# A layer step on one core: first product behind the second transposes, row factors inside the first unit's product, x differences on VectorE

## Chip, cores and metric

The kernel runs on one core of one Trainium2 chip. The metric is the device time of one execution in microseconds; three runs of the kernel before gave 2393.43, 2394.09 and 2395.15 us, so its median is 2394.09 us. One more execution was taken by the hardware profiler, and all rows that are shown come from it.

The engines are named as the profile names them: PE (TensorE matmuls, with PEld for its weight loads), DVE (VectorE), ACT (ScalarE), POOL (GpSimd) and SP (SyncE, which here only issues DMAs). A name with a q behind it (SPq, ACTq) is the engine's instruction queue.

## What is computed

One layer of a hybrid encoder over 512 prompt frames and 64 sample frames, so T = 576 frames of width 2048:

```python
hn = rmsnorm(x, g_norm1)
q, k, v, gb, gc, hc = split(hn @ w_in)           # 2048 x 6144
q, k = rmsnorm(q, g_q), rmsnorm(k, g_k)          # per head of 128
o_attn = stick_breaking(q, k, v)                 # 8 heads, cached keys for the sample
o_conv = gb * conv3_causal(gc * hc)
x = x + concat(rmsnorm(o_attn), rmsnorm(o_conv)) @ w_out
h2 = rmsnorm(x, g_norm2)
x = x + (silu(h2 @ w_gate) * (h2 @ w_up)) @ w_down
```

The outputs are x, the new key and value rows, and the last two rows of gc * hc. Everything is f32. Each f32 matmul is done as three matmuls of rounded halves (hi*hi, lo*hi, hi*lo), which is why every operand is split by a cast (ACT) and a subtraction (DVE).

## The kernel before

Frames lie along the free dimension in two halves of 288. The norm of the first layer is applied late: the products run on x times g_norm1 alone, and each result is multiplied by R1, a [128, 576] tile that holds 1/rms of every frame in all partitions ("row factors").

The change concerns the first 100 us, the input projection's start. It has three stages.

Stage one, the loop over `kt` from 0 to 18 (lines 674 to 704). For each of the 16 row blocks of x, `turn_x(kt)` turns the loaded x by four transposes on PE into a PSUM bank `psx` (banks z0 and z1 in turn), and the sample frames by small transposes into `psx_s` (bank "misc"); ACT copies them to `st`, and ACT and DVE make the hi and lo operands b11, b12 and bod, scaled by g_norm1 (`g1c`). `step0(0, v0ps, kt - LAG)` is the product of pass kt - 3: twelve matmuls, into four PSUM banks (three of "pj", one of z2), of the columns of two value heads. Its weights come in four quarters (`load_wv`), split by `split_wv`: a cast on ACT, a subtraction on DVE. `x_sums` (lines 574 to 588) makes four differences of x's quarters for the later products, three on DVE and one (t2) on POOL; `x_parts` splits them into t12a and t34a. `x_squares` sums the squares for the norm.

Stage two, the second loop over `kt` from 0 to 15 (lines 721 to 753): `step0(1, v1ps, kt)` for two further value heads, into banks z0, z1 and the two of "misc", beside what is left of x_squares, x_sums and x_parts. At kt 9 the squares become 1/rms (`rst`, a power on POOL); at kt 11 five diagonal tiles `dg` are made from it on DVE; at kt 13, ahead of that pass's matmuls in PE's order, `turn_vectors` turns the small vectors and five f32 matmuls of a matrix of ones with `dg` spread 1/rms over all partitions into `ps_r`, which DVE copies to R1.

Stage three, the units. A unit is a 256-column piece of a product, done by seven half-size products (numbers 1 to 7) from sums of weight quarters and sums of frame quarters. Weights of a unit come as two halves into raw_a and raw_b; `weight_sums` makes four sums of them on DVE (lines 348, 350, 352, 354), and `prepare` splits one operand `whl` by a cast on ACT (line 231) and a subtraction on DVE (line 232), four products ahead. `run(n, p)` does product p of unit n: 24 matmuls in eight steps, and after each step `pipe.tick()` lets waiting generators go on. `tokens` is such a generator: it turns a finished value tile E back into token rows by PE transposes into "misc" (tok_a, four transposes, then tok_b, one), copied by ACT and stored by SP. E0 and E1 are the value tiles of stages one and two, multiplied by R1 on DVE ahead of `tokens`. The first units are -22 and -21 (-NA and 1 - NA in the code), and the order of the first products is (-22,1), (-22,2), (-21,1), (-21,2), (-22,3), (-22,6), (-22,5).

What sets the order: PE's instructions stand in the order of the code throughout. In stages one and two ACT, DVE and SP do too. In stage three a scheduler orders ACT, DVE, POOL and SP when the kernel is built; each engine then runs its list in order. In the list of the kernel before, ACT copies the token rows of both E1 tiles ahead of the two `whl` casts that need the weight sums of lines 352 and 354. In the list of the changed kernel these two casts, and the cast of x_sums' b11, stand ahead of the first token copy, and the scaling of the two E0 tiles stands between the sums of lines 350, 352 and 354 on DVE.

Pools hand out their buffers in turn: "misc" has two, so the third token transpose waits until ACT has copied the first; "hl" has three, and holds the x differences and the token rows alike.

## Time and profile before

| | us |
|---|---|
| runs: median (lowest to highest) | 2394.09 (2393.43 to 2395.15) |
| the profiled execution | 2397.15 |
| its span, first to last instruction | 2395.4 |
| PE busy | 2350.2 (98%) |
| DVE busy | 1934.0 (81%) |
| ACT busy | 1234.6 (52%) |
| POOL busy | 300.3 (13%) |
| mean granted TensorE clock | 0.995 |

Timeline rows give the start, the duration, the engine, the line, the operation, the tile written and the tiles read, the shape, and how many instructions are merged; in brackets stands how long the engine had been idle before it and what ended that. Durations include the drain of an instruction, so the start of the next one on the same engine gives the pace. The rows of a table by stretches give, for each engine, the busy time and in brackets the instructions, then the granted TensorE clock, the share of the DMA engines, and GB/s.

### The profile page before, as it was taken

To read this page: it belongs to the slowest core of one execution; us is meant where nothing else is said; L and a number is where in the kernel's file an instruction comes from. 1 tells how busy PE (TensorE), PEld (TensorE's weight loads), DVE (VectorE), ACT (ScalarE), POOL (GpSimd) and SP (SyncE) were. 2 spreads that over 40 slices of the span, in tenths; PEclk is the share of its full clock that TensorE was granted. 3 is DMA by queue.
4 is the path that set the end of the run, shared out by engine and by line. 5 is a ranking of instruction groups with operands and counts; after the bars stand their busy time and mean duration, and the time that the engine had idled before them with its cause. 6 is when DMAs were issued, how large, how long until landed. Compare 5 with 4: busy or idle time off the path is not lost.

```text
span 2395.4 us, 43789 instructions
## 1 busy us (share of the span) xinstructions
PE 2350.2 (98%) x17609; PEld 2336.2 (98%) x17609; DVE 1934.0 (81%) x2828; ACT 1234.6 (52%) x2211; POOL 300.3 (13%) x377
## 2 busy tenths in 40 slices
PE   8899999999999999999999999999999899999998
PEld 8899999999899999999999999999999899999998
DVE  7888888787677768888888888888888768887875
ACT  7456656455777545444444444444444444444454
POOL 0111121120233221000000000000000002431211
PEclk9999999999999999999999999999999999999999
DMA  7433343525733333444444444345354936875642
GB/s 254 141 113 104 114 138 89 162 88 188 236 105 104 107 135 106 141 150 132 139 151 142 129 150 153 118 156 159 109 157 139 338 111 212 225 222 194 204 129 79
DMA packets 474900, 360.60 MB, mean 151 GB/s; under 512 B 11278, under 2 KB 460680, under 8 KB 474696
## 3 DMA queue, kind: packets, MB, share of 16 engines
q1 hardware_dynamic: 469528, 351.02, 45.8%
q0 software_dynamic: 5168, 6.79, 1.6%
q8 instruction: 138, 2.26, 0.4%
q14 instruction: 66, 0.54, 0.1%
HBM read 281.39 MB, written 76.37 MB: 149 GB/s over the span
## 4 chain that ended last, share of the span: by engine, by line
PE 82%; DVE 6%; ACT 4%; issue 2%; DMA 1%; POOL 1%; SPq 0%; DVEq 0%; ACTq 0%; POOLq 0%
PE psy L406 43%; PE psw L406 21%; PE psx L406 10%; PE pjo L227 5%; DVE whl L232 1%; DMA v_dram<-tok 1%; PE pw L1391 1%; ACT whl L231 1%; ACT ph L231 0%; PE pot L1514 0%; DVE c L881 0%; ACT whi L179 0%; DMA raw_a<-in_w_down_dram 0%; DVE raw_b L350 0%; DVE wlo L180 0%
## 5 line engine op out<-in xcount | busy, mean ns | idle before, releaser
L232 DVE TENSOR_TENSOR whl<-raw_a,whl 128x1024 fp32r<-128x1024 f32 (+4 forms) x376 | 424.6, 1130 | 70.2 <-ACT whl L231 68.5
L406 PE MATMUL psy<-t,whl 128*128 128x288 f32 x2916 | 437.3, 295 | 0.5 <-ACT part L429 0.5
L231 ACT CAST whl<-raw_a 128x1024 fp32r<-128x1024 f32 (+4 forms) x376 | 352.3, 938 | 141.4 <-PE psx L406 52.1
L406 PE MATMUL psy<-h_s,whl 128*128 128x288 f32 x2724 | 411.8, 295 | 6.8 <-ACT part L429 6.8
L406 PEld LDWEIGHTS psy<-t,whl 128*128 128x128 f32 x2916 | 403.4, 189 | 0.9 <-ACT part L429 0.7
L406 PEld LDWEIGHTS psy<-h_s,whl 128*128 128x128 f32 x2724 | 378.7, 189 | 7.3 <-ACT part L429 7.3
L406 PE MATMUL psw<-t,whl 128*128 128x288 f32 x2592 | 377.2, 295 | 0.0
L406 PEld LDWEIGHTS psw<-t,whl 128*128 128x128 f32 x2592 | 354.0, 189 | 0.2
L232 DVE TENSOR_TENSOR whl<-raw_b,whl 128x1024 fp32r<-128x1024 f32 (+5 forms) x230 | 247.7, 1077 | 89.3 <-ACT whl L231 87.8
L231 ACT CAST whl<-raw_b 128x1024 fp32r<-128x1024 f32 (+5 forms) x230 | 207.2, 903 | 208.2 <-PE psw L406 70.0
L429 ACT COPY part<-psy 128x288 f32<-128x288 f32 x303 | 120.8, 399 | 350.0 <-PE psy L406 345.4
L406 PE MATMUL psx<-h_s,whl 128*128 128x288 f32 x1122 | 166.8, 297 | 2.7 <-DVE gs L1371 2.7
L406 PEld LDWEIGHTS psx<-h_s,whl 128*128 128x128 f32 x1122 | 156.2, 191 | 2.9 <-issue 2.9
L231 ACT CAST whl<-s 128x1024 fp32r<-128x1024 f32 (+5 forms) x101 | 93.3, 924 | 119.9 <-PE psw L406 114.1
L406 PE MATMUL psy<-t12a,whl 128*128 128x288 f32 x1056 | 150.0, 295 | 2.0 <-ACT part L429 2.0
L406 PE MATMUL psw<-t34a,whl 128*128 128x288 f32 x1056 | 150.4, 295 | 1.4 <-DVE ghs L869 0.9
L406 PEld LDWEIGHTS psy<-t12a,whl 128*128 128x128 f32 x1056 | 143.2, 188 | 2.7 <-ACT part L429 2.7
L406 PEld LDWEIGHTS psw<-t34a,whl 128*128 128x128 f32 x1056 | 143.4, 188 | 1.9 <-DVE ghs L869 1.1
L232 DVE TENSOR_TENSOR whl<-s,whl 128x1024 fp32r<-128x1024 f32 (+5 forms) x101 | 107.5, 1065 | 19.9 <-ACT whl L231 18.1
L227 PE MATMUL pjo<-mixc,whi 128*128 128x288 f32 x512 | 119.4, 300 | 0.0
L1334 POOL DMA_DIRECT2D hid_dram<-form x3 | 2.4, 807 | 923.9 <-DVE form L232 923.9
L227 PE MATMUL pjo<-mixa,whi 128*128 128x288 f32 x512 | 102.7, 295 | 0.0
(599 smaller groups left out, 4138.4 us busy)
## 6 DMA issues: line engine op xcount, KB each, us to landing
hid_dram<-form SPq DMA_DIRECT2D x147, 288.0 KB, 2.3
raw_a<-in_w_gate_dram SPq DMA_DIRECT2D x23, 1024.0 KB, 6.4
raw_a<-in_w_up_dram SPq DMA_DIRECT2D x23, 1024.0 KB, 6.0
raw_a<-in_w_in_dram SPq DMA_DIRECT2D x22, 1024.0 KB, 5.5
raw_b<-in_w_in_dram SPq DMA_DIRECT2D x22, 1024.0 KB, 8.2
raw_b<-in_w_gate_dram SPq DMA_DIRECT2D x21, 1024.0 KB, 6.7
raw_b<-in_w_up_dram SPq DMA_DIRECT2D x21, 1024.0 KB, 7.8
h_s<-hid_dram SPq DMA_DIRECT2D x10, 2016.0 KB, 9.9
```

The source lines that it names most:

```text
L227: mm(ps, w_[:, k, csl], x_[:, a:b], start=(k == 0 and n == 0), stop=(k == nk - 1 and n == 2))
L231: cast = nc.scalar.copy(out=hi, in_=src)
L232: (lo_eng or nc.vector).tensor_tensor(out=lo, in0=src, in1=hi.bitcast(F32), op=ALU.subtract)
L406: mm(ps, whl[:, w_, j, :], x_, start=(start and j == 0 and q == 0), stop=(j == len(xs_) - 1 and q == 2), skip_group_check=True)
L429: nc.scalar.copy(out=t, in_=st["y"])
L1334: q.dma_start(out=hid_dram[fp][2 * n - 2 : 2 * n].rearrange("f p t -> p f t"), in_=t.bitcast(F32))
L1391: mm(pss[j, i], w_[:, k, j * P : (j + 1) * P], x_, start=(kk == 0 and k == 0 and n == 0), stop=(kk == 1 and k == 7 and n == 2))
```

## The change

The diff, cut to its core:

```diff
--- before.py
+++ after.py
...
@@ -531,10 +532,10 @@
...
-    def load_s(c):
+    def load_s(c, queue=nc.sync):
         t = tmp.tile([P, 2, HALF], F32, tag="hl", name="xsn", bufs=3).rearrange("p i t -> p (i t)")
         xsn[c] = t[:TS, : 4 * P]
-        nc.sync.dma_start(out=xsn[c], in_=xs[:, 4 * c * P : 4 * (c + 1) * P])
+        queue.dma_start(out=xsn[c], in_=xs[:, 4 * c * P : 4 * (c + 1) * P])
 
     stp = {}
     banks = {}
@@ -543,15 +544,19 @@
         j, q = divmod(kt, 2)
         c = next(c for c, (k0, k1) in enumerate(XCH) if k0 <= kt < k1)
         k = kt - XCH[c][0]
+        psx = ps_z.tile([P, 512], F32, tag=f"z{kt % 2}", name=f"psx{kt}")
+        for i in range(4):
+            nc.tensor.transpose(psx[:, i * P : (i + 1) * P], xin[c][:, i, k * P : (k + 1) * P], ident)
         if kt % 8 == 0:
             banks["s"] = misc("psx_s")
         if kt % 4 == 0:
             for s in range(4):
                 o = (kt % 8 + s) * TS
                 nc.tensor.transpose(banks["s"][:, o : o + TS], xsn[kt // 4][:, s * P : (s + 1) * P], ident[:TS, :TS])
-        psx = ps_z.tile([P, 512], F32, tag=f"z{kt % 2}", name=f"psx{kt}")
-        for i in range(4):
-            nc.tensor.transpose(psx[:, i * P : (i + 1) * P], xin[c][:, i, k * P : (k + 1) * P], ident)
+        if kt == 0:
+            psg = misc("ps_g1")
+            nc.tensor.transpose(psg[:, :KD], g1raw, ident[:KD, :KD])
+            nc.vector.tensor_copy(out=g1c, in_=psg[:, :KD])
         if q == 0:
             stp[j] = ypool.tile([P, 2, T], F32, tag=f"y{j}", name=f"st{j}")
         st = stp[j]
@@ -582,7 +587,7 @@
         ta, tb = (tmp.tile([P, 2, HALF], F32, tag=tag, name="tab", bufs=3 if tag == "hl" else 2) for _ in range(2))
         t1, t2, t3, t4 = ta[:, 0], ta[:, 1], tb[:, 0], tb[:, 1]
         nc.vector.scalar_tensor_tensor(out=t1, in0=ev[:, HALF:], scalar=ge, in1=b11s, op0=ALU.mult, op1=ALU.subtract)
-        nc.gpsimd.tensor_tensor(out=t2, in0=b22s, in1=t1, op=ALU.subtract)
+        nc.vector.tensor_tensor(out=t2, in0=b22s, in1=t1, op=ALU.subtract)
         nc.vector.scalar_tensor_tensor(out=t3, in0=ev[:, HALF:], scalar=ge, in1=b22s, op0=ALU.mult, op1=ALU.subtract)
         nc.vector.scalar_tensor_tensor(out=t4, in0=od[:, :HALF], scalar=go, in1=t2, op0=ALU.mult, op1=ALU.subtract)
         tabs[j] = ta, tb
@@ -623,22 +628,29 @@
         def raw0(q):
             return raw_tile["A"][:, q // 2, q % 2 * 1024 : (q % 2 + 1) * 1024]
 
-        def load_wv(v, q):
+        def load_wv(v, q, a=0, b=4):
             c0 = 2 * AW + 2 * v * P
-            nc.sync.dma_start(out=raw0(q).rearrange("p (k c) -> p k c", k=4),
-                              in_=w_in[4 * q * P : 4 * (q + 1) * P, c0 : c0 + 2 * P].rearrange("(k p) c -> p k c", p=P))
-
-        def split_wv(v, q):
-            if q % 2 == 0:
+            nc.sync.dma_start(out=raw0(q).rearrange("p (k c) -> p k c", k=4)[:, a:b],
+                              in_=w_in[(4 * q + a) * P : (4 * q + b) * P, c0 : c0 + 2 * P]
+                              .rearrange("(k p) c -> p k c", p=P))
+
+        def split_wv(v, q, a=0, b=4):
+            if q % 2 == 0 and a == 0:
                 wv[v, q // 2] = [wpool.tile([P, 2048], F32R, tag=tag, name=tag) for tag in ("whi", "wlo")]
-            hi, lo = (t[:, q % 2 * 1024 : (q % 2 + 1) * 1024] for t in wv[v, q // 2])
-            split(hi, lo, raw0(q))
+            a, b = 256 * a, 256 * b
+            hi, lo = (t[:, q % 2 * 1024 : (q % 2 + 1) * 1024][:, a:b] for t in wv[v, q // 2])
+            if v == q == a == 0:
+                nc.vector.tensor_copy(hi, raw0(q)[:, a:b])
+                nc.vector.tensor_tensor(out=lo, in0=raw0(q)[:, a:b], in1=hi.bitcast(F32), op=ALU.subtract)
+            else:
+                split(hi, lo, raw0(q)[:, a:b])
 
         load_x(0)
-        load_s(0)
-        nc.sync.dma_start(out=g1raw, in_=g_norm1[0].rearrange("(r c) -> r c", c=P))
+        load_s(0, nc.scalar)
+        nc.scalar.dma_start(out=g1raw, in_=g_norm1[0].rearrange("(r c) -> r c", c=P))
+        load_wv(0, 0, 0, 2)
         load_x(1)
-        load_wv(0, 0)
+        load_wv(0, 0, 2, 4)
         load_x(2)
         load_s(1)
         load_x(3)
@@ -674,11 +686,12 @@
         for kt in range(KD + LAG):
             if kt < KD:
                 if kt == 0:
-                    psg = misc("ps_g1")
-                    nc.tensor.transpose(psg[:, :KD], g1raw, ident[:KD, :KD])
-                    nc.vector.tensor_copy(out=g1c, in_=psg[:, :KD])
+                    split_wv(0, 0, 0, 2)
                 turn_x(kt)
-            if kt in (0, 4, 8, 12):
+                if kt == 1:
+                    split_wv(0, 0, 2, 4)
+                    step0(0, v0ps, 0)
+            if kt in (4, 8, 12):
                 split_wv(0, kt // 4)
             if kt in (2, 6, 10, 14):
                 square(xsn[kt // 4], ssx[:TS, 4, kt // 4 : kt // 4 + 1], nc.scalar)
@@ -700,8 +713,8 @@
                 x_sums(j, "e" if j < 2 else "hl")
             if kt in (9, 13):
                 x_parts((kt - 9) // 4)
-            if kt >= LAG:
-                step0(0, v0ps, kt - LAG)
+            if kt == 3 or kt > 4:
+                step0(0, v0ps, 1 if kt == 3 else kt - LAG)
         e0 = [e_tile(f"E0{c}") for c in range(2)]
         for c in range(2):
             for i, (a, b) in enumerate(HALVES):
@@ -710,8 +723,8 @@
                 else:
                     nc.vector.tensor_copy(out=e0[c][:, a:b], in_=v0ps[c][i])
         x_parts(2)
-        v1ps = [[ps_z.tile([P, 512], F32, tag=f"z{i}", name="pjz")[:, :HALF] for i in range(2)],
-                [misc("pjm")[:, :HALF] for i in range(2)]]
+        v1ps = [[(ps_z.tile([P, 512], F32, tag=f"z{c + 1}", name="pjz") if c == i else misc("pjm"))[:, :HALF]
+                 for i in range(2)] for c in range(2)]
         load_columns([("A", 0)])
         R1 = rpool.tile([P, T], F32, tag="R", name="R1", bufs=2)
 
@@ -729,28 +742,42 @@
                 nc.vector.reduce_sum(out=ssr, in_=ssx, axis=mybir.AxisListType.X)
                 nc.vector.tensor_scalar(out=ssr, in0=ssr, scalar1=1.0 / D, scalar2=EPS, op0=ALU.mult, op1=ALU.add)
                 nc.gpsimd.tensor_tensor(out=rst, in0=ssr, in1=nhalf, op=ALU.pow)
-            if kt in (2, 5, 8, 11, 14):
-                x_parts(3 + (kt - 2) // 3)
-            if kt == 11:
-                dg = [hl_tile("dg") for _ in range(2)]
-                dg = [dg[i // 4][:, i % 4 * P : i % 4 * P + n] for i, (_, n) in enumerate(row_pieces())]
-                for i, (_, n) in enumerate(row_pieces()):
-                    nc.vector.tensor_scalar(out=dg[i][:n], in0=ident[:n, :n], scalar1=rst[:n, i : i + 1], scalar2=None,
-                                            op0=ALU.mult)
-            if kt == 13:
-                turn_vectors(ps_pj.tile([P, 512], F32, tag="pj", name="ps_vec"))
-                psr = [ps_pj.tile([P, 512], F32, tag="pj", name="ps_r1") for _ in range(2)]
-                for i, (o, n) in enumerate(row_pieces()):
-                    mm(psr[i // 4][:, o % TP : o % TP + n], oner.bitcast(F32)[:n, :], dg[i][:n], start=True, stop=True)
-                nc.vector.tensor_copy(R1[:, :TP], psr[0])
-                nc.vector.tensor_copy(R1[:, TP:], psr[1][:, :TS])
-            if kt in (1, 4, 7, 10, 13):
+            if kt in (3, 6, 9, 12):
+                x_parts(3 + (kt - 3) // 3)
+            if kt in (1, 4, 7, 10):
                 x_sums(3 + (kt - 1) // 3, "hl")
             if kt == 10:
                 prepare(-NA, 1)
-            if kt == 15:
+            if kt == 13:
+                dg = hl_tile("dg")
+                for i, (o, n) in enumerate(row_pieces()):
+                    nc.vector.tensor_scalar(out=dg[:n, o : o + n], in0=ident[:n, :n], scalar1=rst[:n, i : i + 1],
+                                            scalar2=None, op0=ALU.mult)
                 prepare(-NA, 2)
             step0(1, v1ps, kt)
+
+    def first_scale():
+        yield 5
+        psr, psv = (ps_pj.tile([P, 512], F32, tag="pj", name=name) for name in ("ps_r1", "ps_vec"))
+        for i, (o, n) in enumerate(row_pieces()):
+            mm(psr[:, o : o + n] if i < 4 else psv[:, P : P + n], oner.bitcast(F32)[:n, :], dg[:n, o : o + n],
+               start=True, stop=True)
+        nc.vector.tensor_copy(R1[:, :TP], psr)
+        nc.vector.tensor_copy(R1[:, TP:], psv[:, P : P + TS])
+        e1 = [lpool.tile([P, UW - 2], F32, tag=f"c{c}", name="E1")[:, :T] for c in range(2)]
+        for c in range(2):
+            for i, (a, b) in enumerate(HALVES):
+                nc.vector.tensor_tensor(out=e1[c][:, a:b], in0=v1ps[c][i], in1=R1[:, a:b], op=ALU.mult)
+            pipe.spawn(tokens(e1[c], vp[:, 2 + c, :], vs[:, 2 + c, :], v_dram[2 + c], 8 + 5 * c))
+        turn_vectors(psv)
+        yield 6
+        x_sums(7, "hl")
+        yield 3
+        x_parts(7)
+        yield 12
+        for c in range(2):
+            nc.vector.tensor_tensor(out=e0[c], in0=e0[c], in1=R1, op=ALU.mult)
+            pipe.spawn(tokens(e0[c], vp[:, c, :], vs[:, c, :], v_dram[c], 8 + 8 * c))
 
     def tokens(E, dst, dst_s, dram, lag):
         yield lag
...
@@ -908,16 +934,9 @@
                                        op0=ALU.mult, op1=ALU.subtract)
         nc.sync.dma_start(out=mixc_dram[g][:, :, a:b], in_=m.bitcast(F32))
 
-    e1 = [lpool.tile([P, UW - 2], F32, tag=f"c{c}", name="E1")[:, :T] for c in range(2)]
-    for c in range(2):
-        for i, (a, b) in enumerate(HALVES):
-            nc.vector.tensor_tensor(out=e1[c][:, a:b], in0=v1ps[c][i], in1=R1[:, a:b], op=ALU.mult)
-        pipe.spawn(tokens(e1[c], vp[:, 2 + c, :], vs[:, 2 + c, :], v_dram[2 + c], 4 + 5 * c))
+    pipe.spawn(first_scale())
     raw_tile["B"] = lpool.tile([P, 2, 2048], F32, tag="rb", name="raw_b")
     load_columns([("B", 0), ("B", 1)])
-    for c in range(2):
-        nc.vector.tensor_tensor(out=e0[c], in0=e0[c], in1=R1, op=ALU.mult)
-        pipe.spawn(tokens(e0[c], vp[:, c, :], vs[:, c, :], v_dram[c], 24 + 8 * c))
 
     order = [(-NA, 1), (-NA, 2), (1 - NA, 1), (1 - NA, 2), (-NA, 3), (-NA, 6), (-NA, 5), (1 - NA, 3), (-NA, 7), (-NA, 4),
              (1 - NA, 6), (1 - NA, 5), (1 - NA, 7), (2 - NA, 1), (1 - NA, 4), (2 - NA, 2), (2 - NA, 6), (2 - NA, 7),
```

On PE, `psx` is turned ahead of `psx_s`, and the turning of g_norm1 moves behind both. On SP the first x_sample load and g_norm1 are gone (ACT's queue issues them), and the first weight quarter comes in two pieces. On DVE the first half of that quarter is split whole, ahead of g1c; the t2 of all eight `x_sums` is done there instead of on POOL. Passes 0 and 1 of the first product stand behind the transposes of row blocks 1 and 3 (before: behind 3 and 4); from pass 2 on the order is as before. The second product uses bank z2 in place of z0. The last `x_sums` and `x_parts` (row blocks 14 and 15), the spreading of 1/rms, the turning of the vectors, and the scaling of E1 and E0 move behind the first 18 matmuls of product (-22,1), or later. On SP the load of raw_a for unit -20 stands ahead of the token stores instead of behind eight of them. Behind the first 120 us the lists of all engines are alike.

## Prediction before the run

> **What bounds the kernel now.** I read the page's busy table first, then the busy times by stretches of 5 us, and the timeline of PE, DVE, ACT, POOL and SP over the first 145 us.
>
> ```profile
> PE 2350.2 (98%) x17609; PEld 2336.2 (98%) x17609; DVE 1934.0 (81%) x2828; ACT 1234.6 (52%) x2211; POOL 300.3 (13%) x377
> ...
> 65.00:70.00 5.00, 1.71 (x14) 1.45 (x12) 3.52 (x8) 3.26 (x6) 2.17 (x2) 0.91 0.42 117
> 70.00:75.00 5.00, 3.25 (x12) 2.91 (x13) 3.93 (x13) 0.63 (x2) 0.37 (x3) 0.50 0.98 294
> ```
>
> PE is busy for 98% of the span, so only PE's idle and slow time can be won. All that the change touches lies ahead of 120 us; there the two stretches from 65 to 75 us (busy us of PE, PEld, DVE, ACT and POOL, then PE's clock, DMA share, GB/s) stand out (1.71 and 3.25 us busy of 5, clock 0.91 and 0.50). The timeline shows the hole:
>
> ```profile
> 45.80 0.30 PE L671 MATMUL pjz<-b,whi 128*128 128x288 f32 x1
> ...
> 66.44 0.27 PE L262 MATMUL ps_vec<-ident,vecs 128*128 128x128 f32 x1
> 71.75 2.69 PE L744 MATMUL ps_r<-dg,oner 128*128 128x128 f32 x10 [5.03 <-DVE dg L738]
> ...
> 79.92 2.15 PE L406 MATMUL psy<-b,whl 128*128 128x288 f32 x15
> ```
>
> Stage two runs from 45.80. Its first 13 passes end at 66.44, 1.588 us each. Then PE waits 5.03 us for `dg`, does the five f32 matmuls of ps_r at half clock (2.6 us), and reaches product (-22,1) at 79.92. Sixteen passes at that pace are 25.4 us, so without the hole the product would start at 71.2. What PE waits for:
>
> ```profile
> 68.50 0.52 DVE L587 SCALAR_TENSOR_TENSOR tab<-st,g1c,tab 128x288 f32<-128x288 f32 x1 [1.44 <-POOL tab L585]
> ...
> 71.41 1.02 DVE L738 TENSOR_SCALAR dg<-ident,vecs 128x128 f32<-128x128 f32 x5
> ```
>
> `dg` stands on DVE behind x_sums steps that wait for their t2 on POOL; the last waited 1.44 us, the power being ahead of it there. The second hole is at the start:
>
> ```profile
> 4.93 0.26 PE L678 MATMUL ps_g<-ident,vecs 16*128 16x16 f32 x1 [4.93 <-DMA vecs<-in_g_norm_dram]
> ...
> 5.73 1.97 PE L554 MATMUL psx<-ident,xin 128*128 128x128 f32 x8
> 10.45 1.94 PE L554 MATMUL psx<-ident,xin 128*128 128x128 f32 x8 [2.75 <-DMA xin<-in_x_prompt_dram]
> 12.04 0.59 PE L671 MATMUL pj<-b,whi 128*128 128x288 f32 x1
> ...
> 14.92 0.46 PE L551 MATMUL psx_s<-ident,xsn 64*128 64x64 f32 x4
> ...
> 19.48 0.60 PE L554 MATMUL psx<-ident,xin 128*128 128x128 f32 x4
> ```
>
> After the transposes of blocks 0 and 1, PE waits 2.75 us for x of blocks 2 and 3 (10.45), with the first product's operands nearly made.
>
> **The change, part by part.** The sum is made against the profiled execution, 2397.15 us (span 2395.4 plus 1.75 around it); it was 3.06 us above the median of the runs, and I carry gains over to 2394.09.
>
> *First pass into the hole.* Pass 0 (12.04 to 14.92, 2.88 us at half clock) moves ahead of the transposes of blocks 2 and 3. Its operands come in time: g_norm1's turning started at 4.93 before, and now g1c waits on DVE for the split of the weights' first half (copy and subtraction of 512 columns, about half of the 1.21 us of a 1024-column row each, below), so it comes about 1 us later; ACT's casts and DVE's subtractions of 0.5 us each follow, and pass 0 should run from about 7 to 9.9. What x of blocks 2 and 3 is late by is bytes, and these are the same; two issues fewer on SP gain it at most 0.6 us. From 10.45 to the turning of block 6 at 19.48 are 9.03 us with three passes in them; two stay. If pass 1 then takes the cold place of pass 0, what is saved is a warm pass, 1.6 us; if pass 0 has already warmed the clock, it is 2.9 plus 0.8, half of the eight transposes' 1.59. With x 0 to 0.45 us earlier and pass 0 up to 1 us late, the ends are 0.6 and 4.1. I take 2.6, near the middle, since the clock will turn at a moment that no row fixes. From block 6 on the order of PE is unchanged, and ACT and DVE hang on PE there, so it all shifts. Cost of the extra DVE work: none, DVE has only that to do then; uncovered it would be 1.2 us.
>
> *t2 on DVE.*
>
> ```profile
> 47.32 0.52 DVE L587 SCALAR_TENSOR_TENSOR tab<-st,g1c,tab 128x288 f32<-128x288 f32 x1 [0.69 <-POOL tab L585]
> ...
> 106.44 0.46 DVE L858 TENSOR_TENSOR c<-c,R 128x288 f32<-128x288 f32 x1
> ```
>
> DVE now waits 0.69 for POOL in each x_sums and will work about 0.45 instead (the row of line 858, same size). It gains some 0.24 us each, five times by `dg`, and 0.75 more where the power stood ahead: 2 us. PE needs `dg` later than it did: three passes (4.8) and 18 of 24 matmuls of a product (2.4). From 5.0 late, `dg` comes to be 4.2 early, and the old hole is gone: T1, the start of (-22,1), comes at 71.2 - 2.6 = 68.6, a gain of 11.3 us over 79.92. Bounds: 9.3 to 12.8.
>
> *What first_scale puts into the unit.* On PE it is the same ps_r group as before, now warm, half of 2.6 us plus the vectors' transpose: 1.4 us. But the token transposes of E1 now follow at once, and what they wait for is long. DVE first:
>
> ```profile
> 66.64 2.13 SPq L331 DMA_DIRECT2D raw_b<-in_w_in_dram  x2
> ```
>
> raw_b can be loaded when pass 12 has read b12a, as before. Both megabytes were in by 75 us: 5 us at 117 GB/s and 5 at 294, in the stretches above, are 2055 KB. The first was in at 70 + (1048 - 585)/294 = 71.6, 5.1 us behind pass 12. That makes it T1 + 0.3. DVE's list stands in the order: sum of line 348, two `whl`, R1, four E1, the vectors, line 350, E0, line 352, E0, line 354.
>
> ```profile
> 73.86 0.69 DVE L745 COPY R<-ps_r 128x512 f32<-128x512 f32 x1 [1.04 <-PE ps_r L744]
> 74.47 0.23 DVE L746 COPY R<-ps_r 128x64 f32<-128x64 f32 x1
> ...
> 77.85 0.75 DVE L919 TENSOR_TENSOR E<-E,R 128x576 f32<-128x576 f32 x1
> ...
> 79.19 1.21 DVE L232 TENSOR_TENSOR whl<-raw_a,whl 128x1024 fp32r<-128x1024 f32 x1
> 80.32 0.81 DVE L914 TENSOR_TENSOR E<-pjz,R 128x288 f32<-128x288 f32 x2
> ...
> 85.30 1.23 DVE L350 TENSOR_TENSOR raw_b<-raw_b,raw_a 128x1024 f32<-128x1024 f32 x1
> 86.56 1.23 DVE L352 TENSOR_TENSOR raw_a<-s,raw_a 128x1024 f32<-128x1024 f32 x1
> ...
> 88.07 1.22 DVE L354 TENSOR_TENSOR raw_a<-raw_a 128x1024 f32<-128x1024 f32 x1
> ```
>
> By starts: line 348 like line 350, 1.26, and two `whl` of 1.13 from T1 + 0.3 give 3.8 (ps_r is done at 3.5); R1 0.75; four E1 1.46; vectors 0.4; lines 350, 352 and 354 1.26 + 1.14 + 1.13; two E0 of 0.67. Line 354 ends at T1 + 11.3. Behind it on ACT stand the `whl` cast, b11s and only then the first token copy:
>
> ```profile
> 69.68 0.53 ACT L580 ACTIVATE b11s<-st,g1c 128x288 f32<-128x288 f32 x1
> ...
> 82.54 0.59 ACT L761 COPY tok<-tok_a 128x512 f32<-128x512 f32 x1 [0.55 <-PE tok_a L759]
> ...
> 87.88 1.05 ACT L231 CAST whl<-raw_a 128x1024 fp32r<-128x1024 f32 x1 [1.23 <-DVE raw_a L352]
> ```
>
> Before, the copy (82.54) stood ahead of the cast that waits for line 352 (87.88). Now it follows both casts and b11s: 11.3 + 1.0 + 0.5 + 0.6 = T1 + 13.4. PE needs that copy for the third turn into "misc", the tokens of the other E1 tile, and gets there much sooner:
>
> ```profile
> 74.37 0.61 PE L671 MATMUL pjz<-bod,whi 128*128 128x288 f32 x1
> ...
> 81.91 0.60 PE L759 MATMUL tok_a<-ident,E 128*128 128x128 f32 x4
> ...
> 87.38 3.37 PE L406 MATMUL psy<-b,whl 128*128 128x288 f32 x24
> ```
>
> A product is 3.2 us: 24 matmuls at 0.133, the pace within the row at 87.38. Two of them, the ps_r group, one tok_a (0.4 by starts) and nine matmuls of a third with tok_b (1.3) make T1 + 9.5. **PE waits 3.9 us there.** Next it waits for tok_b: ACT's copy of the former stands behind the casts of the last x_parts, and these behind t2 and t4 on DVE, which follow two more `whl`: 11.3 + 2.3 + two c 0.9 + the four of x_sums 2.0, a subtraction 0.75 and the copy make about T1 + 17.2, a further wait of 1 to 2 us. Six matmuls of (-21,1) are then left; before, that point (0.8 ahead of the end of the row at 87.38, so 89.8) lay 9.9 behind 79.92. So 17.2 - 9.9 = 7.3 us of the 11.3 are given back. Bounds: 6.0 without the E0 tiles in between, and 10.4 if raw_b takes 8.2 us instead of 5.1, the median of its loads:
>
> ```profile
> raw_b<-in_w_in_dram SPq DMA_DIRECT2D x22, 1024.0 KB, 8.2
> ```
>
> Later I see no further loss: from (-22,6) on DVE has the same distance to PE as before, and both shift alike.
>
> *The clock.* A wait costs more than itself:
>
> ```profile
> 947.31 0.55 PE L406 MATMUL psy<-h_z,whl 128*128 128x288 f32 x3
> 950.52 5.38 PE L406 MATMUL psx<-h_s,whl 128*128 128x288 f32 x21 [2.66 <-DVE gs L1371]
> ```
>
> The same stretch in busy times:
>
> ```profile
> 949.50:950.00 0.50, 0.00 (x0) 0.00 (x0) 0.50 (x3) 0.00 (x0) 0.00 (x0) 0.76 1.09 394
> ...
> 956.50:957.00 0.50, 0.50 (x5) 0.50 (x5) 0.34 (x1) 0.34 (x1) 0.00 (x0) 0.91 0.00 0
> ```
>
> After 2.66 us of waiting the clock fell at about 949.8 and came back at 956.55, so PE ran 6.0 us at half speed and lost 3.0. A wait of 2.19 us did not do it:
>
> ```profile
> 561.09 0.75 PE L805 MATMUL ssg<-accc,oner 128*128 128x288 f32 x2 [2.19 <-DVE yt L792]
> ```
>
> The new wait of 3.9 is above both, and the second wait lies so near that the clock cannot recover in between. I take 2.4 us, less than 3.0 since some of the slow time passes inside the second wait; ends 0 and 3.4. [...]
>
> *Other edits.* Banks z1, z2 and "misc" for the second product: z2 is free once ACT has copied E0, early in the first pass; nothing. raw_a's load ahead of the token stores on SP: nothing unless the stores are late (a rival). POOL's eight t2 gone: nothing, it was idle.
>
> **Sum:** 11.3 - 7.3 - 2.4 = 1.6 us gained. 2394.09 - 1.6 = **2392.5**.
>
> **Rivals.**
>
> *No new wait.* If the sums are done before PE wants the tokens, only the ps_r group stays: 11.3 - 1.4 = 9.9 us, 2384.2. For it: DVE is ahead of PE at T1 by the count above, and the same token copies cost PE nothing before. Against: ACT's list, and four us of DVE work too many.
>
> *Token stores late (slower).* SP now issues 1 MB of raw_a at about T1 + 14 ahead of the token stores.
>
> ```profile
> 94.81 6.48 DMA v_dram<-tok
> ```
>
> A store behind such a load took 6.48 us. ACT's copy of the second tok_b needs the buffer of the first store, and ahead of PE's next turn there are 2 us to spare (T1 + 15 + 6.5 = 21.5, against 17.2 + 0.8 + 3.2 + 2.9 = 24.1). If raw_b is late by 3.1 and the store has to follow a raw_a load of 8.2, the copy comes at 17.2 + 8.2 + 6.5 = T1 + 31.9 against 27.2: 4.7 us more, with 3.1 for raw_b and another 2.4 of slow clock 10.2 in all: 2402.7. It decides once a store takes over 9.1 us.
>
> *The first pass does not fit.* If the weights' first half lands late (7 us), g1c and pass 0 are, and the transposes of blocks 2 and 3 stand behind: the early gain is 0, 2395.1.
>
> **How the numbers follow.** My forecast has 0.55, no new wait 0.25, late stores 0.15, no early gain 0.05. A measurement of this kernel tells about 0.2%, 4.8 us, from no change. Faster: the whole of the second and 0.1 of the forecast (early gain at its upper end, short waits), 0.35; slower: 0.15; within: 0.50. The forecast's own range is 2388 to 2396.5. To leave out no more than 2 in 10, 2384 to 2397.5 is needed: it ends at the first rival's time, and leaves the late stores out.
>
> **What would show it.** Right: product pass 0 ahead of 10 us; no wait for `dg`, (-22,1) from about 69 us; a wait of 3 to 5 us at the third token turn, ended by ACT's copy of the first, which follows casts that wait for lines 352 and 354; the clock at 0.50 for some 6 us around 80 to 90. Wrong: no wait above 1 us between 65 and 100 (the first rival), one at a tok_b that a store ends (the second), or a changed pace behind 120 us, which I exclude.

## The result, and the profile after

The changed kernel takes 2392.16 us in the median of 21 executions, the kernel before 2395.15 us in 21 beside it: a ratio of 0.9987 with a 95% interval of 0.9982 to 0.9993, or 1.7 to 4.3 us less. The profiled execution is one at the median: 2392.16 us, its span 2390.5. The 0.2% at which the prediction drew its line are 4.8 us, so this counts as no change there. Executions of one kernel differ by more than the change does: of 76 of the kernel before, run beside the experiments, the 36 with a mean granted PE clock of 0.996 or more have a median of 2393.26 us and the 40 with less one of 2396.94, and the two groups overlap.

The timeline of PE in the changed kernel (start, busy time, engine, line, operation and tile; in brackets the idle time before the group and what ended it):

```profile
5.69 0.69 PE L555 MATMUL psx_s<-ident,xsn 64*128 64x64 f32 x4 [0.70 <-DMA xsn<-in_x_sample_dram]
...
8.12 0.61 PE L683 MATMUL pj<-b,whi 128*128 128x288 f32 x1 [0.20 <-ACT b L570]
...
11.24 1.91 PE L549 MATMUL psx<-ident,xin 128*128 128x128 f32 x8
...
69.46 2.55 PE L406 MATMUL psy<-b,whl 128*128 128x288 f32 x18
...
74.71 0.33 PE L262 MATMUL ps_vec<-ident,vecs 128*128 128x128 f32 x1 [1.45 <-DVE R L766]
...
83.14 0.66 PE L786 MATMUL tok_a<-ident,E 128*128 128x128 f32 x4 [2.38 <-ACT tok L788]
87.44 0.33 PE L795 MATMUL tok_b<-ident,E 128*128 128x128 f32 x1 [2.45 <-ACT tokz L797]
...
88.48 4.82 PE L406 MATMUL psx<-bod,whl 128*128 128x288 f32 x24
...
101.31 3.48 PE L406 MATMUL psy<-t12a,whl 128*128 128x288 f32 x24 [0.49 <-ACT part L429]
```

The first pass runs from 8.12, ahead of the transposes of blocks 2 and 3 (11.24; 10.45 before), where PE stood still before. Product (-22,1) starts at 69.46 instead of 79.92, with no wait for `dg`. In place of that one wait stand three: 1.45 us at the vectors' transpose, 2.38 at the third token turn into "misc" and 2.45 at its tok_b. Two rows show where it ends: the 24 matmuls at 88.48 take 4.82 us in place of 3.37, and product (-22,5), the mark used below, starts at 101.31, where before it started at 102.01. Of the 10.5 us won at (-22,1), 0.7 are left at the mark.

The busy times by stretches of 5 us (PE, PEld, DVE, ACT, POOL; then PE's granted clock, DMA share, GB/s) show the same from the side:

```profile
80.00:85.00 5.00, 2.61 (x19) 2.14 (x18) 5.00 (x8) 2.55 (x4) 0.00 (x0) 1.00 0.02 4
85.00:90.00 5.00, 2.56 (x14) 2.56 (x15) 2.70 (x4) 3.48 (x6) 0.94 (x1) 0.83 1.03 316
```

PE is busy for little over half of these ten microseconds, DVE for all of the first five, and the clock falls behind the waits. What stands ahead of them is read from DVE and ACT:

```profile
66.86 1.02 DVE L754 TENSOR_SCALAR dg<-ident,vecs 128x128 f32<-128x128 f32 x5
...
70.42 1.23 DVE L348 TENSOR_TENSOR s<-raw_b 128x1024 f32<-128x1024 f32 x1 [1.41 <-DMA raw_b<-in_w_in_dram]
...
76.22 1.21 DVE L350 TENSOR_TENSOR raw_b<-raw_b,raw_a 128x1024 f32<-128x1024 f32 x1
...
78.08 1.22 DVE L352 TENSOR_TENSOR raw_a<-s,raw_a 128x1024 f32<-128x1024 f32 x1
...
79.89 1.22 DVE L354 TENSOR_TENSOR raw_a<-raw_a 128x1024 f32<-128x1024 f32 x1
```

```profile
79.55 1.05 ACT L231 CAST whl<-raw_a 128x1024 fp32r<-128x1024 f32 x1 [3.29 <-PE psx L406]
81.14 1.04 ACT L231 CAST whl<-raw_a 128x1024 fp32r<-128x1024 f32 x1 [0.54 <-DVE raw_a L354]
82.09 0.53 ACT L585 ACTIVATE b11s<-st,g1c 128x288 f32<-128x288 f32 x1
82.53 0.56 ACT L788 COPY tok<-tok_a 128x512 f32<-128x512 f32 x1
...
87.12 0.27 ACT L797 COPY tokz<-tok_b 128x128 f32<-128x128 f32 x1 [0.61 <-DVE t12a L232]
```

The weight sums of lines 350, 352 and 354 end at 77.4, 79.3 and 81.1; ACT's casts stand right behind the last two (the first of them waits last for PE's product (-22,2), the second for the sum of line 354), then b11s, and only then, at 82.53, the copy of the first token turn. PE resumes when it has ended. The copy of tok_b (87.12) follows the casts of the last x forms and waits 0.61 us more for DVE's subtraction of t12a, whose buffer of "hl" it takes over.

### The profile page after: what moved, and what is told of

It is laid out like the page before. It is cut to its first block, busy times and chain, and to the rows that moved or that the text cites. A ratio compares the mean times of both kernels' runs of the same rounds, so it can differ in the third digit from the quotient of the medians.

```text
span 2390.5 us, 43793 instructions
## 1 busy us (share of the span) xinstructions
PE 2348.5 (98%) x17609; PEld 2334.4 (98%) x17609; DVE 1937.0 (81%) x2838; ACT 1234.0 (52%) x2211; POOL 293.9 (12%) x369
## 4 chain that ended last, share of the span: by engine, by line
PE 85%; DVE 7%; ACT 4%; issue 2%; POOL 1%; DMA 1%; SPq 0%; DVEq 0%; ACTq 0%; POOLq 0%
PE psy L406 43%; PE psw L406 22%; PE psx L406 10%; PE pjo L227 5%; DVE whl L232 1%; PE pj L683 1%; PE pjz L683 1%; ACT whl L231 1%; PE pjm L683 1%; PE pw L1410 1%; ACT ph L231 0%; ACT whi L179 0%; PE pot L1533 0%; DVE c L907 0%; DMA out_dram<-tok 0%
```

## The experiments

The mark is the start of product (-22,5). T1 is the start of (-22,1), and "behind T1" is counted from there, so that what the first part of the kernel does is kept apart from the first unit. Each kernel was timed beside the kernel before on its chip: the changed one in 21 executions, the version with the factors on ACT behind the copies in 6 and 5, the others in 11.

| kernel | median, us | ratio to before (95%) | T1 | mark | mark behind T1 |
|---|---|---|---|---|---|
| before, profile | | | 79.92 | 102.01 | 22.09 |
| changed | 2392.16 | 0.9987 (0.9982 to 0.9993) | 69.46 | 101.31 | 31.85 |
| changed, again | 2393.15 | 0.9989 (0.9980 to 0.9998) | 68.80 | 100.66 | 31.86 |
| early part alone | 2392.10 | 0.9994 (0.9985 to 1.0002) | 77.72 | 99.75 | 22.03 |
| the rest alone | 2395.49 | 1.0003 (0.9994 to 1.0012) | 71.31 | 101.58 | 30.27 |
| vectors later | 2388.24 | 0.9975 (0.9966 to 0.9984) | 68.76 | 96.56 | 27.80 |
| copies first | 2389.46 | 0.9976 (0.9967 to 0.9985) | 69.22 | 93.89 | 24.67 |
| copies first, factors on ACT | 2387.52 | 0.9970 (0.9958 to 0.9981) | 68.31 | 91.96 | 23.65 |
| the same, again | 2386.55 | 0.9964 (0.9951 to 0.9976) | 69.44 | 93.06 | 23.62 |
| warm | 2392.01 | 0.9991 (0.9982 to 1.0000) | 67.93 | 98.24 | 30.31 |
| t2 on POOL | 2393.33 | 0.9991 (0.9982 to 1.0000) | 69.42 | 101.75 | 32.33 |
| vectors later, factors on ACT | 2389.53 | 0.9976 (0.9967 to 0.9985) | 69.00 | 98.60 | 29.60 |

### The early part alone

The kernel before with the diff's parts for `load_s`, `turn_x`, `load_wv`, `split_wv` and the first loop:

```
+                    step0(0, v0ps, 0)
...
-            if kt >= LAG:
-                step0(0, v0ps, kt - LAG)
+            if kt == 3 or kt > 4:
+                step0(0, v0ps, 1 if kt == 3 else kt - LAG)
```

> Only the early part of the change (first pass behind the transposes of blocks 0 and 1, half weights, two loads on ACT's queue) in the kernel before; stage two and the first unit as before. The mark is the start of product (-22,5), 102.01 us before and 101.31 after. Theory: the early part is worth about 1.7 us by the start of stage two (44.1 instead of 45.8); ACT and DVE hang on PE there, so dg shifts as well, the wait for dg stays at 5 us, (-22,1) starts at about 78.2, the mark is at 100.3, the time 1.7 us below before (ratio 0.9993). Rival: DVE's work up to dg is set by loads, which do not move: the wait for dg grows to 6.7 us, the mark stays at 102.0, ratio 1.000.

PE's timeline:

```profile
63.91 0.27 PE L262 MATMUL ps_vec<-ident,vecs 128*128 128x128 f32 x1
69.22 2.69 PE L756 MATMUL ps_r<-dg,oner 128*128 128x128 f32 x10 [5.04 <-DVE dg L750]
```

The wait for `dg` is 5.04 us, as it was (5.03), only everything is 2.5 us sooner: the vectors' transpose stands at 63.91, where it stood at 66.44. The theory holds, with 2.2 us at T1 and 2.3 at the mark instead of 1.7 (the other 0.3 went in slow passes behind the wait; the granted clock is 0.86 from 60 to 70 us and 0.80 from 70 to 80). DVE's work up to `dg` follows PE; the rival, that it follows the loads, is out.

### The rest alone

The other parts of the diff in the kernel before: t2 on DVE, the banks, `dg` and the x forms later, `first_scale`.

> The change without its early part: t2 on DVE, other banks, the row factors and last x forms in the first unit. Theory: no wait for dg, (-22,1) at 71.2; raw_b's load, the sums and with them both token waits hang on pass 12, so everything is 1.7 us later than in the changed kernel: waits of 2.4 and 2.4 us at the second tok_a and the first tok_b, mark at 103.0, 1 us later than before, ratio 0.9995 to 1.0010. Rival: the token waits are set by something fixed in time (the load's arrival), they shrink by 1.7 us, and the mark is at 101.3 as in the changed kernel.

```profile
76.51 0.33 PE L262 MATMUL ps_vec<-ident,vecs 128*128 128x128 f32 x1 [1.40 <-DVE R L754]
...
84.95 0.66 PE L774 MATMUL tok_a<-ident,E 128*128 128x128 f32 x4 [2.38 <-ACT tok L776]
...
89.25 0.33 PE L783 MATMUL tok_b<-ident,E 128*128 128x128 f32 x1 [2.45 <-ACT tokz L785]
...
90.21 3.37 PE L406 MATMUL psx<-bod,whl 128*128 128x288 f32 x24
```

T1 is at 71.31, 25.4 behind the start of stage two in this run (45.92; 45.80 before): the hole is gone without the early part. The waits are those of the changed kernel (1.40, 2.38 and 2.45 for 1.45, 2.38 and 2.45), so they hang on the lists and not on a fixed time. But the mark is at 101.58, not 103.0: here the clock did not fall (1.00 from 80 to 100 us), the 24 matmuls at 90.21 take 3.37 us. Between that tok_b and the mark lie 12.3 us here and 13.9 in the changed kernel (87.44 to 101.31): the slow clock cost 1.5 us there. By the marks the early part is worth 2.3 us alone and the rest 0.4; by the times neither part alone is clear of no change (0.9985 to 1.0002, 0.9994 to 1.0012).

### The vectors' transpose later

```
-        turn_vectors(psv)
         yield 6
+        turn_vectors(psv)
         x_sums(7, "hl")
```

> The changed kernel with the vectors' transpose 6 ticks later in the first unit, so that PE does not wait for DVE's copies of the row factors (1.45 us). Theory: that wait goes, but PE only comes sooner to the second tok_a, whose bank hangs on ACT's copy behind the weight casts: that wait grows from 2.4 to 3.8 us and the mark stays at 101.3 within 0.4; ratio to the changed kernel 1.000. Rival: the 1.45 us are PE's own loss: mark at 99.9.

```profile
81.20 1.12 PE L786 MATMUL tok_a<-ident,E 128*128 128x128 f32 x4 [2.60 <-ACT tok L788]
81.97 2.38 PE L406 MATMUL psy<-b,whl 128*128 128x288 f32 x9
84.19 0.27 PE L795 MATMUL tok_b<-ident,E 128*128 128x128 f32 x1
```

Neither came. The wait of 1.45 us is gone, the one at the second tok_a is 2.60 instead of 3.8, and the one at tok_b is gone too; the mark is 27.8 behind T1, 4.05 sooner, though the clock fell here too (2.38 us for nine matmuls, 0.66 from 80 to 85 us). My expectation left out that the order of ACT and DVE in the unit is not written out but planned: with the transpose moved, the plan put the x sums ahead of the two E0 products on DVE and the casts of the x forms sooner on ACT. ACT's list in this kernel:

```profile
80.57 0.58 ACT L788 COPY tok<-tok_a 128x512 f32<-128x512 f32 x1
...
83.29 0.27 ACT L797 COPY tokz<-tok_b 128x128 f32<-128x128 f32 x1
```

The first token copy (80.57) comes 1.3 us sooner behind T1 than in the changed kernel, the copy of tok_b (83.29) 3.1 sooner. So this run does not tell PE's own 1.45 us apart from the lists.

### The token copies first

Casts and subtractions of the products (-22,3) and (-22,6), the last x sums and the vectors' transpose are written behind both token turns of E1, and ACT keeps the written order over four products:

```
+        yield 1
         turn_vectors(psv)
-        yield 6
+        yield 16
+        prepare(*order[4])
+        prepare(*order[5])
         x_sums(7, "hl")
-        yield 3
+        yield 5
         x_parts(7)
-        yield 12
...
+        if k_ == 0:
+            hand = ExitStack()
+            hand.enter_context(tc.manual_schedule(engines={mybir.EngineType.Activation}))
         run(n, p_, n in early)
-        if k_ + 4 < len(order):
+        if k_ == 3:
+            hand.close()
+        if 1 < k_ < len(order) - 4:
             prepare(*order[k_ + 4])
```

> The changed kernel with the casts of product (-22,3) and (-22,6), the last x sums and the vectors' transpose put behind both E1 token turns, and ACT's order kept as written there. Theory (the token waits come from ACT's list, where the first copy stands behind casts that wait for the weight sums): both waits of 2.4 us go, the clock stays at 1.00 from 75 to 100 us, the mark is at 93 to 96 us, ratio to before 0.996 to 0.9975. Rival (DVE is full from 70 to 88 us, so the waits only move): PE waits as long at product (-22,3) or (-22,6) for its operand, the mark is at 99 to 102, ratio as the changed kernel's, 0.9987.

```profile
74.49 0.33 PE L262 MATMUL ps_vec<-ident,vecs 128*128 128x128 f32 x1 [0.89 <-DVE R L766]
...
79.97 0.60 PE L788 MATMUL tok_a<-ident,E 128*128 128x128 f32 x4
...
93.89 3.47 PE L406 MATMUL psy<-t12a,whl 128*128 128x288 f32 x24 [0.49 <-ACT part L429]
99.16 3.44 PE L406 MATMUL psv<-bod,whl 128*128 128x288 f32 x24 [1.81 <-ACT part L429]
...
107.48 3.48 PE L406 MATMUL psw<-t34a,whl 128*128 128x288 f32 x24 [1.70 <-DVE ghs L897]
```

No wait is left at a token turn (79.97 has no bracket), the clock is 1.00 from 60 to 130 us, and the mark is at 93.89. The weight sums come no sooner for it (line 354 starts 10.6 us behind T1, 10.4 in the changed kernel), so the two waits were ACT's list. The ratio, 0.9976, lies just outside what was expected (0.996 to 0.9975), since the rival gets its share later: product (-21,3) waits 1.81 us and (-22,4) 1.70, where 0.49 and 0.85 stood, so 2.2 of the 5.6 us (30.3 less 24.7 behind T1) are lost again. The version with the vectors later, whose mark is 2.7 us later, was 1.2 us faster in the median; the intervals of the two overlap, so the times do not rank them.

### The row factors on ACT besides

Against the version with the copies first:

```
-        nc.vector.tensor_copy(R1[:, :TP], psr)
-        nc.vector.tensor_copy(R1[:, TP:], psv[:, P : P + TS])
+        nc.scalar.copy(out=R1[:, :TP], in_=psr)
+        nc.scalar.copy(out=R1[:, TP:], in_=psv[:, P : P + TS])
...
-        yield 16
+        yield 13
...
-        yield 5
+        yield 6
```

> The version with the E1 token copies first, with two things more: the row factors are copied from PSUM by ACT, which is idle there, and the casts for (-22,3) and (-22,6) stand one token copy earlier in ACT's list. Second mark: the start of product (-21,5), 120.54 us before, 119.88 after, 114.61 in the version without the two. Theory (behind the token waits DVE decides, full from 70 to 97 us): 0.9 us of DVE copies and about 1 us of its waiting for ACT's casts go, the wait of 0.89 us of the vectors' transpose goes, the waits of 1.81 and 1.70 us at (-21,3) and (-22,4) shrink to 0.5 to 0.9, and the second mark comes at 112 to 113; ratio to before 0.9960 to 0.9972. Rival (those two waits are set by something else, as the load of the next columns): they stay, the second mark is at 113.7 to 114.6.

```profile
97.00 3.48 PE L406 MATMUL psv<-bod,whl 128*128 128x288 f32 x24 [1.56 <-ACT part L429]
...
105.17 3.43 PE L406 MATMUL psw<-t34a,whl 128*128 128x288 f32 x24 [1.53 <-DVE ghs L897]
...
112.27 3.46 PE L406 MATMUL psy<-t12a,whl 128*128 128x288 f32 x24 [0.49 <-ACT part L429]
```

The second mark is at 112.27, inside 112 to 113, but the two waits only shrank to 1.56 and 1.53. Counted from T1 it is 1.4 us sooner (43.96 for 45.39): 0.9 of that is the vectors' transpose, which no longer waits, and 0.4 the two waits. What ends the wait at (-21,3) is ACT's copy of the part, which stands behind a cast that waits for the sum of line 354, so DVE is the next bound:

```profile
94.65 1.05 ACT L231 CAST whl<-raw_a 128x1024 fp32r<-128x1024 f32 x1 [2.75 <-DVE raw_a L354]
...
96.55 0.39 ACT L429 COPY part<-psy 128x288 f32<-128x288 f32 x1
```

This is the fastest version: 2387.52 us here and 2386.55 in a second comparison, in which the changed kernel took 2393.15 on the same chip.

> The version with the token copies first and the row factors copied by ACT, once more, beside the changed kernel on one chip: 4 to 6 us faster than it in the median, mark (start of (-22,5)) 23.4 to 24.0 us behind the start of (-22,1), no wait at a token turn.

The difference there is 6.6 us, a little over the 4 to 6 expected; the mark was 23.62 behind T1.

### Keeping PE busy in the waits

```
+        if lag == 13 and dram is not None:
+            warm(15)
         pa = misc("tok_a")
...
+        if lag == 13 and dram is not None:
+            warm(15)
         pb = misc("tok_b")
```

`warm(k)` issues k matmuls of 288 columns into a bank of their own.

> The changed kernel with 15 matmuls whose result nobody reads ahead of the second tok_a and of its tok_b (2.0 us each in a spare bank), so that PE works while it would wait; nothing is left out. Theory: the lists of the other engines are the same, both banks come free when they did, PE idles under 0.6 us at each place, the clock stays at 1.00 from 75 to 100 us, and the mark (start of (-22,5)) comes 30.3 us behind the start of (-22,1), as in the run without the early part, in place of 31.85 in the changed kernel's profile; the time falls by at most 1.5 us, ratio to before 0.9980 to 0.9988. Rival (the slow stretch around 87 to 94 us is no consequence of idling): the clock falls all the same, the mark 31.8 us behind.

```profile
79.09 2.17 PE L787 MATMUL warm<-b,oner 128*128 128x288 f32 x15
81.62 0.66 PE L792 MATMUL tok_a<-ident,E 128*128 128x128 f32 x4 [0.36 <-ACT tok L794]
...
85.93 0.33 PE L803 MATMUL tok_b<-ident,E 128*128 128x128 f32 x1 [0.43 <-ACT tokz L805]
...
86.89 3.37 PE L406 MATMUL psx<-bod,whl 128*128 128x288 f32 x24
```

PE works through 2.17 us of each wait and idles 0.36 and 0.43; the banks come free at 13.69 and 18.00 behind T1, as in the changed kernel (13.68 and 17.98). The clock stays at 1.00 from 75 to 100 us, the matmuls at 86.89 take 3.37 us, and the mark is 30.31 behind T1. That the slow stretch follows from idling is not shown by this one profile, since the run of the rest alone kept the clock through its whole waits. In the time nothing shows: 0.9991 here, 0.9987 and 0.9989 for the changed kernel, with intervals of 0.0005 to 0.0009 on either side.

### t2 on POOL again

```
-        nc.vector.tensor_tensor(out=t2, in0=b22s, in1=t1, op=ALU.subtract)
+        nc.gpsimd.tensor_tensor(out=t2, in0=b22s, in1=t1, op=ALU.subtract)
```

> The changed kernel with t2 of x_sums on POOL again. Theory: dg is needed 4 us later than it is there, so 2 us more on DVE's way to it cost nothing at ps_r; DVE's waiting of 1.41 us for raw_b takes up most of what is late, and in the unit t2 costs 0.3 more: the marks are 0 to 0.8 us later relative to the start of (-22,1), ratio to before 0.998 to 0.9995. Rival: without t2 on DVE dg is late again, PE waits for it 1 us or more at ps_r, and the marks are 2 us later or more.

DVE's timeline ahead of the unit, and PE's where it uses `dg`:

```profile
68.25 1.02 DVE L754 TENSOR_SCALAR dg<-ident,vecs 128x128 f32<-128x128 f32 x5
...
70.56 1.23 DVE L348 TENSOR_TENSOR s<-raw_b 128x1024 f32<-128x1024 f32 x1 [0.16 <-DMA raw_b<-in_w_in_dram]
```

```profile
71.79 1.05 PE L763 MATMUL ps_r<-dg,oner 128*128 128x128 f32 x8
```

`dg` is done at 69.27, 0.15 ahead of T1 (69.42), where the changed kernel has it at 67.88, 1.58 ahead. That is 1.4 us later, and PE asks for it only at 71.79. The waiting for raw_b shrinks from 1.41 to 0.16, so the sums are only 0.2 us later. The mark is 32.33 behind T1, 0.5 later, inside the 0 to 0.8 expected. Moving t2 was worth 1.4 us at `dg`, 0.5 at the mark and nothing that the time shows; the hole stays closed without it, by the later use of `dg`.

### The vectors later and the row factors on ACT

Both edits above in the changed kernel.

> The version with only the vectors' transpose later, and the row factors copied by ACT. Theory: the weight sums, hence ACT's casts and the first token copy, come 0.8 us sooner; the wait at the second tok_a falls from 2.6 to 1.8 us, too short to bring the clock down, and the mark is 25.3 to 26.5 us behind the start of (-22,1) (27.8 in the version without it, slow clock included). Rival: the copy hangs on something else than DVE's list, the wait stays at 2.6.

```profile
80.58 0.66 PE L786 MATMUL tok_a<-ident,E 128*128 128x128 f32 x4 [1.73 <-ACT tok L788]
...
84.92 0.47 PE L795 MATMUL tok_b<-ident,E 128*128 128x128 f32 x1 [2.45 <-ACT tokz L797]
```

The first wait is 1.73, as expected, but the wait at tok_b is back with 2.45 us, and the clock fell at its end (84.70; 0.69 from 85 to 90 us). So the mark is 29.60 behind T1, not 25.3 to 26.5: the expectation missed. The plan had put two `whl` subtractions ahead of the x sums on DVE. A second case of a small edit that shuffles the planned lists.

### The changed kernel again

> The changed kernel once more, for a second profile. [...] Rival: the waits themselves vary by 0.5 us or more.

```profile
82.52 0.66 PE L786 MATMUL tok_a<-ident,E 128*128 128x128 f32 x4 [2.36 <-ACT tok L788]
...
86.81 0.33 PE L795 MATMUL tok_b<-ident,E 128*128 128x128 f32 x1 [2.42 <-ACT tokz L797]
```

Waits of 2.36 and 2.42, the mark 31.86 behind T1, with the slow clock (0.79 from 85 to 90 us; the 24 matmuls behind take 4.88 us): the first unit repeats to 0.1 us. What varies is T1.

## Why the prediction was right

**First pass into the hole.** Right. 2.6 us were forecast (0.6 to 4.1); alone it moved the end of the first 13 passes by 2.5 us (in the changed kernel's first profile stage two starts 1.7 sooner, at 44.07). In the nine profiles of kernels that hold the early part and the later use of `dg` (one has t2 on POOL) T1 lies from 67.93 to 69.46, 68.9 in the mean, for 68.6. The changed kernel's first profile has the latest: its transposes of x_sample waited 0.70 us for their load, which the change moved to ACT's queue (5.69 above). The four profiles with such a wait (0.42 to 0.79) are the four latest, 69.22 to 69.46; the five without lie from 67.93 to 69.00. Pass 0 itself started at 8.12 and not at about 7, so it ended 0.8 us behind the 10.45 at which the transposes of blocks 2 and 3 started before; that is inside the "up to 1 us late" of the bounds. What the prediction calls half clock at pass 0 is the pace of its rows, 0.24 us a matmul by starts and 0.14 from 14.56 on (0.24 up to 11.24, 0.14 from 13.19 on in the changed kernel); the granted clock of these stretches stands as 1.00.

**The hole.** Right: T1 at 71.31 without the early part, for 71.2. The part of it put down to t2 was mis-sized (2 us, measured 1.4) and, as the run with t2 on POOL shows, not needed: `dg` came 4.0 us early for 4.2.

**What first_scale puts into the unit.** Right in its cause and in when the banks come free: T1 + 13.4 and T1 + 17.2 were forecast, 13.7 and 18.0 measured. The waits are shared out otherwise (3.9, and 1 to 2; measured 2.38 and 2.45), since PE came later: the step that failed is the PE side of "on PE it is the same ps_r group as before, now warm". The vectors' transpose writes the bank whose last columns are the row factors' tail, so PE waits 1.45 us until DVE has copied it. I had priced the group at 1.4 us and this wait at nothing. It cost little if PE would have waited at the third turn instead, which no run shows by itself. The give-back is 18.07 - 9.9 = 8.2 us (start of the matmuls behind tok_b, counted from T1) for 7.3, inside its bounds. Three terms of it were too short: raw_b was in at T1 + 0.96 (line 348 at 70.42) and not T1 + 0.3, of which 0.35 are left at the end of line 354 (81.11, T1 + 11.65); the terms for tok_b add up to 17.25 without the copy's 0.27; and DVE's subtraction of t12a ahead of that copy took 1.33 us (85.70) and not 0.75, beside a POOL multiplication (last section).

**The clock.** Right in its place, smaller in size: 1.5 us for 2.4, where it fell, in both profiles of the changed kernel, behind the second wait and not between the two; none in the run of the rest alone, with the same waits. The 2.4 and the sign of "some 6 us" at half clock were taken from the row at 950.52; here it lasted 3.4 us, from 88.29 to 91.70. The step behind the term was wrong: the length of the wait (2.66 did it, 2.19 did not) does not tell whether the clock falls. The wait of 2.19 us at 561.09 stands with 2.18 to 2.20 in five other profiles (558.86 in the early part alone), and there the clock fell, at its end or up to 1.5 us later. What decides was not shown; the last section has what was measured.

**Sum.** The mark was to be 22.09 + 7.3 + 2.4 = 31.8 us behind T1; it is 31.85. Two terms were off by 0.9 each, in opposite ways, so that they meet is luck. So is part of the nearness of 2392.16 to 2392.5: the gain was 3.0 us for 1.6, but the kernel before took 2395.15 in that comparison and not 2394.09.

**The rivals.** No new wait: out, and the kernels with the copies first come nearest to it, with 2386.6 to 2389.5 us for 2384.2; DVE then takes part of it back. Late stores: ACT's second copy of tok_b waited 0.72 us for one in the changed kernel (2.63 in the run with the vectors later, at 93.40), PE for none:

```profile
90.78 0.27 ACT L797 COPY tokz<-tok_b 128x128 f32<-128x128 f32 x1 [0.72 <-DMA v_dram<-tok]
```

First pass not fitting: out; the weights' first half was in at 6.06, when DVE starts on it, and not at 7, and the early part alone is worth 2.2 us at T1.

**The rest of the time.** The time fell by 3.0 us (1.7 to 4.3), the mark by 0.7 in one profile and 1.35 in the other. The remaining 1.6 to 2.3 us were not settled. They are within what the same waits cost later on in one execution and not in another: the wait for `gs`, 2.66 us at 950.52 with a slow clock behind it in the profile of before, is this in the changed kernel's:

```profile
949.60 3.02 PE L406 MATMUL psx<-h_s,whl 128*128 128x288 f32 x21 [2.68 <-DVE gs L1390]
```

2.68 us of waiting, and 21 matmuls at full speed. One pair of profiles is too little for a change of this size: the spans of the pair here differ by 4.9 us, the marks by 0.7, and 2.8 of the 4.2 us between lie at this one wait (0.9 us between the two profiles at its end, 3.7 at 966.71 against 963.02).

## What to carry to other kernels

When a wait is taken away ahead of a stretch where another engine is full, ask at once what that engine owes next: here DVE was full for 11 us ahead of the last weight sum, and 8.2 of the 10.5 us won were gone three products later, 6.3 of them as waits. Read the in-order list of the engine that frees the bank (ACT's), not only the operation that PE waits for: the copy took 0.56 us, what stood ahead of it took three, and the copies written ahead of the casts, with the row factors on ACT, were worth 6.6 us against the changed kernel on one chip, twice the change itself (without the row factors 2.7 by the medians, on different chips). Where a planner fills the lists, an edit of one line can reorder them, so compare the lists before crediting the edit.

## What the runs showed of the hardware

**Waits of one length ended with a slow clock in some executions and not in others.** The waits at the token turns are the same in the changed kernel and in the run of the rest alone (2.38 and 2.45 us). The stretches of 10 us from 80 on, of the changed kernel and then of the other:

```profile
80.00:90.00 10.00, 5.17 (x33) 4.70 (x33) 7.70 (x11) 6.03 (x10) 0.94 (x1) 0.91 0.53 160
90.00:100.00 10.00, 10.00 (x73) 10.00 (x72) 9.06 (x9) 3.77 (x7) 1.65 (x1) 0.92 0.43 135
```

```profile
80.00:90.00 10.00, 5.17 (x40) 4.70 (x39) 9.51 (x13) 5.02 (x8) 0.95 (x2) 1.00 0.33 92
90.00:100.00 10.00, 10.00 (x78) 10.00 (x78) 8.13 (x8) 4.64 (x8) 1.66 (x1) 1.00 0.64 202
```

PE is busy for 5.17 us in the first ten of both, and the granted clock is 0.91 and 0.92 in the one, 1.00 in the other. At 950 it is the same: after 2.66 us of waiting in before the clock is 0.50 from 950 to 955 us, after 2.68 in the changed kernel it is 1.00. In the profile of before, up to its last 10 us, the clock fell at 69.12, in the wait of 5.03 us for `dg`, at 949.76, in the one of 2.66, and at 1885.01, in one of 6.32; in the changed kernel's at 88.29, 0.85 us behind the wait of 2.45, at 617.35, 0.69 behind one of 2.90, and at 1880.28, in one of 6.32. With matmuls that keep PE busy through the token waits, the one profile of that version has a clock of 1.00 from 75 to 100 us. What decides whether the clock falls at a wait of 2 to 3 us no run shows.

**Weight sums that DVE started beside a POOL multiplication took 1.46 to 1.95 us in place of 1.22.** DVE's line 354 takes 1.22 us at 79.89 above; with POOL at work it takes 1.71:

```profile
95.44 1.65 POOL L885 TENSOR_TENSOR c<-c,R 128x288 f32<-128x288 f32 x1 [9.02 <-DVE c L884]
```

```profile
96.47 1.71 DVE L354 TENSOR_TENSOR raw_a<-raw_a 128x1024 f32<-128x1024 f32 x1
```

The sum of line 352 at 95.21, which was on when POOL began, takes its usual 1.22. So it is throughout: in the twelve profiles 168 of the 169 sums of lines 350, 352 and 354 that start during a TENSOR_TENSOR row of POOL take 1.46 to 1.95 us, and the 45 that were on when one began take at most 1.22. To move the E0 products to POOL was not tried.
